# Sums of the out projection's moving operand, made two slices a step beside seventeen attention steps

## The chip, the cores and the metric

The kernel runs on one core of one Trainium2 chip. The metric is the device time of one execution in microseconds (us). Profiles come from the hardware profiler: they name TensorE (PE, with its weight loads as PEld), VectorE (DVE), ScalarE (ACT), GpSimd (POOL) and SyncE (SP), whose queue issues nearly all DMAs of this kernel.

## The reference, cut to what matters

One layer over 2048 tokens of width 1024, all in float32: a token mixer, a cross attention and a feed-forward block, each between two RMS norms. The mixer is what matters here:

```python
u = rms_norm(h, g_mix_pre[l])
z = u @ w_in[l]
qa, ka, va, qh, fh, ih, gh = jnp.split(z, IN_SPLITS, axis=-1)
ya = swa_with_sinks(qa, ka, va, sinks[l])          # sliding-window attention, 8 heads
yh = hgrn2(qh, fh, ih, gh, lb, hgrn_onorm[l])      # gated linear recurrence, 4 heads
y = jnp.concatenate([ya, yh], axis=-1) @ w_out[l]  # the out projection
h = h + rms_norm(y, g_mix_post[l])
```

(The reshapes are left out.) The kernel has to give the same result to within float32 accuracy, so it splits each operand of a large product into a high and a low part and sums three products.

## The kernel before, in words

**Large products.** They run mostly by a scheme that makes seven products of half-size blocks instead of eight (as in Strassen's). For it, sums and differences of the four quarters of the moving operand are needed. For the weights `w_out` of the out projection the program makes these sums once, ahead of time, and stores them in DRAM, in `out_s`; the products' stage later reads them back with `row<-out_s`.

**The sums.** `sums` (L1395) returns the DRAM tile and a generator over `combined` (L1025). For each of two halves of a quarter, `combined` makes four operands (keys 5, 7, 6, 4): it loads halves of the quarters of `w_out` (L75, called from `w_out`, L1388; the upper quarters as two DMAs of 64 partitions), yields three times, makes one `tensor_tensor` of 128 x 1024 on VectorE (L1032), issues the store to `out_s` (L78) and yields once more. That is two halves x four operands x four slices = 32 slices with eight sums, twelve loads of tiles of 512 KB and eight stores of 512 KB. A slice is what one `next` advances. The loads go into tiles `u` (two buffers) and `x` (three buffers) of the pool `io`. The same tiles `u` and `x` hold the decays of the recurrence (L718 to L721, `decays` at L724) for the four columns of the forget gate.

**The order of the work around the change.** Function `mix` interleaves generators by hand. `swa` (L964) gives one attention step of 128 tokens at each `next`, seventeen in all: the front of step n (loads of queries `qd`, keys `kr` and values `vr` from `z_d`, their split, scores, softmax) and the back of step n-1 (transposes, product with the values, store to `y_d`). `hgrn` (L946) gives one pair of chunks of the recurrence. `cols` (`in_proj`, L682) gives one column block of the in projection for the second half of the tokens: 48 matmuls of 128 x 512 (L156 to L158) and an eviction to a tile `z`, which is stored to `z_d`. A first loop of nine turns takes one attention step, one pair of the recurrence and one column each. A second loop takes the remaining eight attention steps and one column each. Then `fold_cross` (the folded weights of the cross attention) runs beside the remaining pairs of the recurrence, and the products begin.

**Who sets the final order.** The program is recorded in this order and then rearranged: the tile framework is asked to schedule the instructions of each engine (`schedule_with_timeline_sim=True`), so that an instruction can be issued earlier or later than the loops name it. What it keeps is the order of dependent instructions and the buffers: a tile of a pool with two buffers waits until the tile two before it is no longer used. Within an engine, and within SP's queue of DMAs, instructions then run strictly in the scheduled order: one that waits holds up all behind it. Queries have two buffers (`qd`, `qs`), keys one (`kr`, `kh`, `kl`).

The names that the text uses: `qs` (L768 on ACT, L769 on DVE) are the split queries; `kh` and `kl` (L987, L988, called at L779) the split keys; L803 and L804 the score matmuls; L808 the masked minimum, L812 the exponential, L823 the normalization; `pth`/`ptl` (L841, L842) the split transposed probabilities, L846 and L847 their product with the values; L732, L738 and L752 the decays.

Of the kernel before, what the change touches and what calls it, by code (L numbers as in the profile page):

```python
# [48 lines left out]
class Layer:  # L49
# [144 lines left out]
    def mix(self):  # L194
        tc, I = self.tc, self.I
        kw = dict(reuse_waits="tile")
        with contextlib.ExitStack() as left:
            def pool(name, at, **k):
                return at.enter_context(tc.tile_pool(name=name, bufs=1, **k, **kw))

            self.mc = pool("mc", left)
            self.r_x = self.cst.tile([P, NT], F32, name="r_x")
            with (
                tc.tile_pool(name="t1", bufs=3, **kw) as self.ts,
                tc.tile_pool(name="t2", bufs=3, **kw) as self.tb,
                tc.tile_pool(name="s1", bufs=2, side="right", **kw) as self.st_pool,
                contextlib.ExitStack() as at,
            ):
                self.banks(at, "ps1", **MOST)
                self.raws = 3  # L210
                u = self.in_first()
            self.banks(left, "ps2", **FOUR)
            self.hg = pool("hg", left)
            self.wp = pool("wp", left)
            self.io = pool("io", left)
            with tc.tile_pool(name="sw", bufs=1, side="right", **kw) as self.sw:
                self.zero_tiles()
                swa = self.swa(range(NT), lambda n: "st" if n < NPB else "sth")
                hgrn = self.hgrn(range(NPB), "h")
                cols = self.in_proj(1, u)  # L220
                next(cols)
                for _ in range(NPB + 1):
                    next(swa)
                    next(hgrn)
                    next(cols)
                for _ in hgrn:
                    pass
                self.out_sums, side = self.sums("out_s", self.w_out, 4, lambda: self.io_tile("u"), lambda: self.io_tile("x"))
                side = side()
                next(side)  # L230
                pairs = self.hgrn(range(NPB, NT), "gt")
                for i, _ in enumerate(swa, NPB + 2):
                    next(cols)
                    if i == NT + 1 - 0:
                        next(pairs)
                    for _ in range(4):
                        next(side, None)
                for _ in cols:
                    pass
            phases = self.phases(self.jobs(), None, lambda: self.io_tile("z"))  # L240
            with tc.tile_pool(name="xp", bufs=1, side="right", **kw) as self.xp:
                fold = self.fold_cross()
                for _ in range(2):
                    next(fold)
                for i, _ in enumerate(pairs, 1):
                    for _ in range(2):
                        next(fold)
                    if 2 <= i < 10:
                        next(phases)
                for _ in fold:  # L250
                    pass
            left.close()
            with (
                tc.tile_pool(name="t3", bufs=3, **kw) as self.ts,
                tc.tile_pool(name="t4", bufs=3, **kw) as self.tb,
                tc.tile_pool(name="s3", bufs=2, side="right", **kw) as self.st_pool,
                contextlib.ExitStack() as at,
            ):
                self.banks(at, "ps3", **MOST)
                self.raws = 4  # L260
                for _ in phases:
                    pass
# [1502 lines left out]
```

## Time and profile before

| what | before |
|---|---|
| median of three runs | 2584.7 us (2578.32 to 2585.96) |
| the profiled execution's own time | 2583.14 us |
| its span, first to last instruction | 2581.4 us |
| mean granted TensorE clock | 0.997 |
| attention with the columns beside it | about 267 to 632 us of the span |
| folded cross attention and remaining recurrence | about 632 to 820 us |

A profile lists instructions by the line of the kernel that made them, the engine, the operation and its tiles (`out<-in`). "Busy" is the union of an engine's instruction spans; matmuls are pipelined, so a busy TensorE may or may not be at its full rate. A wait row names who waited, for whom, the total in us, how often, and the longest. A row of a timeline gives start, duration, engine, line, operation, tiles and count, and in brackets the idle time before it with what ended it. A row of the DMA list gives the count, the size of one and the median time from issue to landing. A row of busy time by stretch gives the stretch, its length, each engine's busy us and count, the granted clock, the mean busy share of the 16 DMA engines and the GB/s they moved.

### The profile page before, as it was taken

What the parts mean: (1) busy time and instruction counts of PE and PEld (TensorE: products, weight loads), DVE (VectorE), ACT (ScalarE), POOL (GpSimd) and SP (SyncE); (2) the same over time, 40 slices, a digit from 0 to 9 for tenths busy, and PEclk for the clock granted to TensorE, in tenths of its full rate; (3) what the DMA queues carried; (4) which work ended last, traced back from release to release, by engine and by line L of the source; (5) the groups of instructions that cost most, each with busy time, mean ns of one, the idle gap of its engine ahead of it and who ended that gap; (6) DMA issues with size and microseconds to landing.
All of it is one profiled execution on the core that took longest, in us unless ns stands there. A gap on an engine that the chain in (4) does not pass through costs nothing.

```text
span 2581.4 us, 34890 instructions
## 1 busy us (share of the span) xinstructions
PE 2540.2 (98%) x12326; PEld 2127.1 (82%) x12326; DVE 1765.3 (68%) x2791; ACT 1262.4 (49%) x2643; POOL 422.6 (16%) x612
## 2 busy tenths in 40 slices
PE   9999999999999999999999999999999999999998
PEld 8888888888988778888778888888888888888886
DVE  7785588987556778778885655566666557574766
ACT  5563466565555565565563333354333335453543
POOL 5231334321302232212300000000000000000022
PEclk9999999999999999999999999999999999999999
DMA  6445755765887886666973622253565425464886
GB/s 188 147 163 178 198 164 158 239 186 175 251 279 283 295 274 217 211 228 200 325 246 127 208 87 74 89 189 130 172 203 196 156 93 190 158 199 106 224 178 152
DMA packets 357295, 486.36 MB, mean 188 GB/s; under 512 B 20352, under 2 KB 248704, under 8 KB 357120
## 3 DMA queue, kind: packets, MB, share of 16 engines
q1 hardware_dynamic: 351072, 462.11, 54.7%
q0 software_dynamic: 6048, 22.02, 4.9%
q8 instruction: 97, 1.59, 0.3%
q14 instruction: 78, 0.64, 0.1%
HBM read 317.34 MB, written 166.72 MB: 188 GB/s over the span
## 4 chain that ended last, share of the span: by engine, by line
PE 83%; DMA 6%; DVE 5%; ACT 3%; issue 2%; SPq 0%; POOL 0%; DVEq 0%; POOLq 0%; ACTq 0%
PE psm L1122 23%; PE psm L1124 23%; PE psm L1123 23%; PE psg L158 2%; PE psg L157 2%; PE psg L156 2%; PE pss L1381 1%; ACT T L985 1%; DMA h1t_d<-row 1%; DMA raw<-in_wo_x_dram 1%; DVE S L988 1%; DMA x<-in_w_out_dram 1%; DMA z<-in_w_out_dram 1%; DMA kk<-z_d 0%; ACT junk L1476 0%
## 5 line engine op out<-in xcount | busy, mean ns | idle before, releaser
L1122 PE MATMUL psm<-T,S 128*128 128x512 f32 x2680 | 1038.3, 392 | 11.4 <-ACT part L1137 9.9
L1123 PE MATMUL psm<-T,S 128*128 128x512 f32 x2680 | 1043.9, 390 | 0.9 <-DVE T L988 0.8
L1124 PE MATMUL psm<-T,S 128*128 128x512 f32 x2680 | 1031.0, 390 | 4.4 <-DVE S L988 4.4
L1122 PEld LDWEIGHTS psm<-T,S 128*128 128x128 f32 x2680 | 504.0, 188 | 120.5 <-ACT part L1137 10.2
L1124 PEld LDWEIGHTS psm<-T,S 128*128 128x128 f32 x2680 | 503.7, 188 | 111.0 <-DVE S L988 6.1
L1123 PEld LDWEIGHTS psm<-T,S 128*128 128x128 f32 x2680 | 504.3, 188 | 105.4 <-DVE T L988 2.3
L985 ACT ACTIVATE S<-sum 128x512 fp32r<-128x512 f32 (+1 forms) x330 | 198.4, 618 | 364.4 <-PE psm L1124 269.5
L988 DVE TENSOR_TENSOR S<-sraw,S 128x512 fp32r<-128x512 f32 (+1 forms) x315 | 214.1, 687 | 227.9 <-ACT S L985 214.2
L988 DVE TENSOR_TENSOR S<-sum,S 128x512 fp32r<-128x512 f32 (+1 forms) x388 | 260.5, 680 | 44.9 <-ACT S L985 29.4
L1137 ACT ACTIVATE part<-psm 128x512 f32<-128x512 f32 x285 | 168.7, 596 | 242.4 <-PE psm L1124 222.6
L985 ACT ACTIVATE S<-sraw 128x512 fp32r<-128x512 f32 (+1 forms) x268 | 165.3, 618 | 105.1 <-PE psm L1124 95.1
L1509 POOL DMA_DIRECT2D y_d<-row x16 | 14.0, 876 | 1076.5 <-DVE row L1695 1025.3
L988 DVE TENSOR_TENSOR T<-row,T 128x1024 fp32r<-128x1024 f32 (+1 forms) x112 | 132.5, 1195 | 40.7 <-ACT T L985 40.4
L157 PE MATMUL psg<-u,whi 128*128 128x512 f32 x320 | 127.8, 399 | 0.0
L158 PE MATMUL psg<-u,wlo 128*128 128x512 f32 x320 | 127.1, 397 | 0.0
L156 PE MATMUL psg<-u,whi 128*128 128x512 f32 x320 | 127.1, 397 | 0.0
L1476 ACT ACTIVATE junk<-row 128x512 f32<-128x512 f32 x160 | 99.7, 624 | 52.3 <-DVE row L1498 31.8
L985 ACT ACTIVATE T<-row 128x1024 fp32r<-128x1024 f32 (+1 forms) x112 | 114.0, 1032 | 17.4 <-DMA row<-d_s 6.6
L987 POOL TENSOR_SCALAR S<-sum 128x512 fp32r<-128x512 f32 x58 | 51.7, 891 | 299.1 <-PE psm L1124 247.1
L1646 DVE TENSOR_TENSOR row<-psm,part 128x512 f32<-128x512 f32 x66 | 43.7, 688 | 68.4 <-PE psm L1124 68.4
L1655 DVE TENSOR_TENSOR part<-psm,part 128x512 f32<-128x512 f32 x66 | 43.8, 688 | 62.7 <-PE psm L1124 62.5
L1695 DVE TENSOR_TENSOR row<-psm,part 128x512 f32<-128x512 f32 x72 | 49.1, 688 | 51.1 <-PE psm L1124 51.0
(364 smaller groups left out, 3710.4 us busy)
## 6 DMA issues: line engine op xcount, KB each, us to landing
sraw<-in_w_gate_dram SPq DMA_DIRECT2D x44, 512.0 KB, 3.6
sraw<-in_w_up_dram SPq DMA_DIRECT2D x44, 512.0 KB, 3.6
hid_d<-row SPq DMA_DIRECT2D x44, 512.0 KB, 2.7
sraw<-hid_d SPq DMA_DIRECT2D x32, 512.0 KB, 4.1
sraw<-in_w_in_dram SPq DMA_DIRECT2D x44, 256.0 KB, 3.4
z_d<-pair SPq DMA_DIRECT2D x20, 512.0 KB, 2.9
raw<-in_w_in_dram SPq DMA_DIRECT2D x20, 512.0 KB, 4.9
z_d<-z SPq DMA_DIRECT2D x20, 512.0 KB, 3.7
```

Source lines behind the costliest of these rows:

```text
L156: nc.tensor.matmul(ps, ah, bh, start=(i == 0), stop=False)
L157: nc.tensor.matmul(ps, ah, bl, start=False, stop=False)
L158: nc.tensor.matmul(ps, al, bh, start=False, stop=(i == n - 1))
L985: self.nc.scalar.activation(hi, raw, AF.Copy)
L987: self.nc.gpsimd.tensor_scalar(hi, raw, 1.0, 1.0, ALU.mult, ALU.mult)
L988: self.nc.vector.tensor_tensor(lo, raw, f32(hi), ALU.subtract)
L1122: nc.tensor.matmul(ps, s[:, 0, k, :], t[:, 0, k, :], start=st, stop=False, **kw)
L1123: nc.tensor.matmul(ps, s[:, 0, k, :], t[:, 1, k, :], start=False, stop=False, **kw)
L1124: nc.tensor.matmul(ps, s[:, 1, k, :], t[:, 0, k, :], start=False, stop=sp, **kw)
L1137: nc.scalar.activation(t, ps, AF.Copy)
L1476: self.nc.scalar.activation(junk, a, AF.Square, scale=float(D) ** -0.5, accum_out=to)
L1695: nc.vector.tensor_tensor(d, a, b, ALU.add)
```

## The change

The generator of the sums is made before the first loop, not between the two loops; it is advanced two slices at each of the nine turns of the first loop (18 slices) and two slices at each turn of the second (the rest), where before it was advanced four slices at each turn of the second loop alone.

```diff
                 cols = self.in_proj(1, u)
+                self.out_sums, side = self.sums("out_s", self.w_out, 4, lambda: self.io_tile("u"), lambda: self.io_tile("x"))
+                side = side()
+                next(side)
                 next(cols)
                 for _ in range(NPB + 1):
                     next(swa)
                     next(hgrn)
+                    for _ in range(2):
+                        next(side, None)
                     next(cols)
                 for _ in hgrn:
                     pass
-                self.out_sums, side = self.sums("out_s", self.w_out, 4, lambda: self.io_tile("u"), lambda: self.io_tile("x"))
-                side = side()
-                next(side)
                 pairs = self.hgrn(range(NPB, NT), "gt")
                 for i, _ in enumerate(swa, NPB + 2):
                     next(cols)
                     if i == NT + 1 - 0:
                         next(pairs)
-                    for _ in range(4):
+                    for _ in range(2):
                         next(side, None)
```

The sums, their loads and stores, and all other work are the same in number and shape. Because two lines are added, every line behind the edit has a number two higher in the changed kernel.

## The prediction

> **What bounds the kernel now.** I read the page first, then busy time by stretch, TensorE's waits in each stretch, and the sums' own rows with the DMA list and SP's timeline. The page's head and its first part:
>
> ```profile
> span 2581.4 us, 34890 instructions
> PE 2540.2 (98%) x12326; PEld 2127.1 (82%) x12326; DVE 1765.3 (68%) x2791; ACT 1262.4 (49%) x2643; POOL 422.6 (16%) x612
> ```
>
> TensorE (PE) is busy for 2540.2 of 2581.4 us. A matmul's span overlaps its neighbour's, so the rate is read from starts:
>
> ```profile
> 449.93 0.39 PE L157 MATMUL psg<-u,whi 128*128 128x512 f32 x1
> 450.16 0.39 PE L158 MATMUL psg<-u,wlo 128*128 128x512 f32 x1
> ```
>
> One 128x512 matmul takes 0.39 us but the next starts 0.23 us later: the column matmuls of the in projection run back to back. The edit keeps every matmul, so it acts only through time in which PE stands still. Busy time by stretch: the attention before the sums, the stretch in which the sums run, the rest of the attention, and the handover to the folded cross attention:
>
> ```profile
> core 0: us, PE busy (x) PEld busy (x) DVE busy (x) ACT busy (x) POOL busy (x), PEclk, DMA share, GB/s
> 267.00:440.00 173.00, 171.72 (x995) 148.81 (x994) 128.81 (x332) 103.12 (x316) 63.62 (x102) 1.00 0.58 169
> 440.00:540.00 100.00, 97.59 (x524) 81.38 (x523) 89.20 (x193) 60.63 (x166) 35.55 (x51) 1.00 0.83 244
> 540.00:632.00 92.00, 90.61 (x489) 76.84 (x487) 71.50 (x183) 54.23 (x143) 13.87 (x29) 1.00 0.44 137
> 632.00:820.00 188.00, 181.04 (x1245) 165.82 (x1246) 103.05 (x138) 100.96 (x224) 39.43 (x50) 1.00 0.81 264
> ```
>
> PE idles 173.00 - 171.72 = 1.28 us, then 100.00 - 97.59 = 2.41, then 1.39, then 6.96. VectorE (DVE) is busy 74% of the first stretch and 89% of the second, where the DMA engines move 244 GB/s instead of 169. So the sums stand in the fuller half, but they disturb PE little there. Who PE waited for from 440 to 540 us, and then from 267 to 440:
>
> ```profile
> PE psh L847 <- DVE ptl L842: 1.0, 2, 0.7
> PE pst L837 <- DVE ptl L842: 0.7, 1, 0.7
> PE pss L837 <- DVE w_mn L808: 0.5, 1, 0.5
> PE pst L837 <- DVE w_mn L808: 0.2, 1, 0.2
> ```
>
> ```profile
> PE pst L804 <- DVE kl L988: 0.7, 1, 0.7
> PE pss L803 <- DVE vst L789: 0.5, 1, 0.5
> ```
>
> All of it is DVE being late: 2.4 us beside the sums, 1.2 us before them.
>
> **The change part by part.** Nothing is added or removed: eight sums (L1032), their loads of w_out and eight stores of out_s move. The sums' own rows, and the row of the stage that reads what they store:
>
> ```profile
> L1032 DVE TENSOR_TENSOR u<-u,x x6: 1207/1221/1225, 451.2 to 525.4; 128x1024 f32<-128x1024 f32 x6
> L1032 DVE TENSOR_TENSOR x<-x,u x2: 1206/1216/1225, 499.2 to 527.1; 128x1024 f32<-128x1024 f32 x2
> ...
> L75 SPq DMA_DIRECT2D row<-out_s x8: 319/352/597, 782.6 to 804.6; - x8
> ```
>
> Eight sums at 1.22 us are 9.8 us of DVE, all of it now between 451 and 527 us. The result is read from 782.6 us on, so no reader is late or early: storing it sooner is worth nothing by itself.
>
> *The late steps.* The order in which the changed program's instructions stand puts three sums beside the first three steps, one at the sixth, one at the eighth or ninth and three around the twelfth. At least four leave the crowded stretch: 4 x 1.22 = 4.9 us, which takes DVE there from 89.2 to about 84.3 of 100. PE's 2.4 us of waiting is the bound of the gain; the other bound is 0, if those waits come from the softmax chain alone. Only half the sums go: I take half, **-1.2 us**.
>
> *The entry.* This is where something gets worse. The changed order places four w_out issues on SP's queue ahead of the first queries, and a fifth, with the first store, ahead of the second step's. SP's timeline at the entry, and the rows that show what issues of w_out take:
>
> ```profile
> 270.84 0.51 SPq L75 DMA_DIRECT2D sg<-z_d  x1
> 271.39 2.66 SPq L75 DMA_DIRECT2D qd<-z_d  x4
> 274.09 1.26 SPq L75 DMA_DIRECT2D kr<-z_d  x2
> 275.40 0.59 SPq L75 DMA_DIRECT2D vr<-z_d  x1
> 278.89 2.58 SPq L75 DMA_DIRECT2D qd<-z_d  x4
> 281.58 0.57 SPq L75 DMA_DIRECT2D kr<-z_d  x1
> ...
> 441.25 1.26 SPq L75 DMA_DIRECT2D x<-in_w_out_dram  x2
> 442.56 1.25 SPq L75 DMA_DIRECT2D u<-in_w_out_dram  x2
> ```
>
> Four issues are 1.26 + 1.25 = 2.5 us, by which the first queries, keys and values come later. What they feed, on DVE (first two rows) and on PE (last two):
>
> ```profile
> 278.18 0.69 DVE L769 SCALAR_TENSOR_TENSOR qs<-qd,qs 64x512 fp32r<-64x512 f32 x1 [7.59 <-ACT qs L768]
> 291.46 0.69 DVE L988 TENSOR_TENSOR kl<-kr,kh 128x512 fp32r<-128x512 f32 x1 [3.78 <-POOL kh L987]
> ```
>
> ```profile
> 281.44 0.33 PE L804 MATMUL pst<-kl,qs 128*128 128x128 f32 x1 [0.73 <-DVE kl L988]
> 294.60 0.28 PE L804 MATMUL pst<-kl,qs 128*128 128x256 f32 x1
> ```
>
> The first score matmuls wait 0.73 us today. In the changed order 68 column matmuls stand ahead of them, not 50: 18 x 0.23 = 4.1 us more cover against 2.5 us more delay, so that wait goes: -0.7. The first sum stands ahead of the first qs on DVE, and queries, keys and scores queue behind it; by a landing time of 5.6 us (row below) its w_out is in at about 271.4 + 2.5 + 5.6 = 279.5, in DVE's idle 7.59 us, and it ends as the shifted qs becomes ready at 278.18 + 2.5 = 280.7: 0, at most 1.2. The cover taken there is missing at the second step: its scores stand behind 96 column matmuls in both orders, and its kl was done at 291.46 + 0.69 = 292.15, 2.4 us ahead of the matmul at 294.60. Delay 2.5 + 0.6 (the fifth issue), less 2.4 of slack, plus the 0.7 by which PE arrives sooner: 1.4. In all **+0.7 us**, between -0.7 (only the first wait goes) and 3.1 + 1.2 = +4.3 (nothing covers).
>
> A rule of the skill speaks against the change here. The Trainium skill, Perfetto Trace Analysis, section "What "DMA-bound" means", counts as DMA-bound a stretch in which the issuing engine's track is solid with DMA slices; SP's rows at the entry have gaps under 0.1 us from 270.84 to 275.99, so it agrees with the form, while PE's single 0.73 us wait there says the bound is still PE.
>
> *The rest of the first nine steps.* A store of out_s waits on SP for its sum, and the next steps' loads wait behind it. SP's and DVE's waits from 440 to 540 us, then the landing times there, then the queries' landing time from 267 to 440:
>
> ```profile
> SPq L78 <- DVE u L1032: 9.9, 4, 4.1
> ```
>
> ```profile
> DVE u L1032 <- DMA out_s<-u: 1.7, 1, 1.7
> ...
> DVE u L1032 <- DMA x<-in_w_out_dram: 0.8, 1, 0.8
> ```
>
> ```profile
> x<-in_w_out_dram SPq DMA_DIRECT2D x12, 256.0 KB, 5.6
> ...
> qd<-z_d SPq DMA_DIRECT2D x18, 128.0 KB, 3.9
> ```
>
> ```profile
> qd<-z_d SPq DMA_DIRECT2D x39, 128.0 KB, 3.2
> ```
>
> In the late steps such stores held SP for 9.9 us in four waits and DVE stood 2.5 us before its sums, and still PE lost only 2.4 us; queries landed in 3.9 us instead of 3.2. The early steps have DVE at 74%, so more slack. I take **0**, between 0 and +9.9 (every held us reaches PE). The tiles u and x are shared with the decays; in the changed order the decay scans keep their places within a step, and their columns are read only from about the twelfth step on, so a late tile costs 0 unless it holds a column's matmuls.
>
> *The handover.* Load order there changes too (k and kk of the next recurrence pairs). It holds PE's largest idle time, 6.96 us; I find no reason for a sign: **0**, between -7.0 and +7.0.
>
> Sum: -1.2 + 0.7 + 0 + 0 = -0.5 us. The profiled execution took 2583.14 us, 2581.4 of it span: 2582.6. The median of the three runs is 1.6 us higher; I state **2583**, between 2582.6 and 2584.7 - 0.5 = 2584.2.
>
> **The rivals.** *SP's issuing bounds the entry.* If the solid SP track is what ends last, all five added issues come through: 5 x 0.63 = 3.2 us, 2586.3 us. For it: the four early issues stand ahead of everything the first step needs. Against it: 18 more column matmuls. (By the rule of the Trainium skill above this would be the result; the trace bears it out in form only.)
>
> *Slower: stores of out_s hold the early steps' loads.* Each of four stores blocks SP's queue until its sum is made, and queries, keys and values of the next step are issued behind it. It decides once a step's loads come later than PE's cover, 2.4 us at the second step. If the 9.9 us measured late reach PE early, the time is 2583.1 + 9.9 = 2593.0, and 4 x 4.1 = 16.4 us at worst, 2599.5. For it: keys have a single buffer, so no step can fetch far ahead. Against it: the late steps, with DVE fuller, let through only a quarter.
>
> *Faster: the disturbance goes with the crowding.* If the late stretch loses all its 2.41 us and the new load order also takes the handover's 6.96, the time is 2583.1 - 9.4 = 2573.7. For it: both stand beside full DMA queues (0.83 and 0.81 busy). Against it: the handover's loads are its own, not the sums'.
>
> *The sums don't move at all*, because the recorded order is rearranged afterwards: excluded, since the first store of out_s stands ahead of the second step's queries in the changed order.
>
> **How the numbers follow.** Forecast 0.51, own range 2578 to 2588 (its terms' bounds, without the held stores and the handover); SP's issuing 0.13; held stores 0.22; faster 0.14. About 0.3% (7.8 us) is what a measurement of this kernel can tell from no change. The forecast and the SP rival lie within it, 0.64; held stores beyond it, 0.22; the faster rival 0.14. The range runs from 2574 (the faster rival's time) to 2598 (held stores, short of their worst) and leaves out about 0.08 below and 0.11 above. Nearly all cases lie close, because PE idles for only 12 us in 553.
>
> **What would show it.** Late steps: DVE from 440 to 540 us at about 84%, PE's wait there near 1.2 us, x<-in_w_out_dram landing faster than 5.6 us. Entry: the first score's wait gone, a new one of 1 to 2 us at the second step's scores. Held stores: waits of SP on L1032 between 270 and 400 us, and PE waits on kl, qs or vst behind them; the forecast fails if these pass 3 us. The handover fails me if PE's idle time from 632 to 820 us differs from 7 us by more than 3. A gain or loss after 820 us would be none of my terms.

## The result, and the profile after

| what | before | after |
|---|---|---|
| median of 10 runs each | 2582.64 us (2577.73 to 2585.96) | 2590.34 us (2585.79 to 2596.99) |
| ratio, 95% interval | | 1.0030 [1.0018, 1.0042] |
| profiled execution, its own time | 2583.14 us | 2591.59 us |
| mean granted TensorE clock in it | 0.997 | 0.995 |

The change costs 7.7 us, 0.3% (by the interval 4.6 to 10.8 us). The ratios in the tables are not quotients of the medians, so that the two can differ by a microsecond or two.

The head of the page after, then its busy time by stretch (columns as in the table of before: PE, PEld, DVE, ACT, POOL busy, granted clock, DMA share, GB/s). Lines behind the edit have numbers two higher: the sum is L1034 now.

```profile
span 2589.9 us, 34898 instructions
...
PE 2546.1 (98%) x12326; PEld 2131.9 (82%) x12326; DVE 1767.1 (68%) x2791; ACT 1260.8 (49%) x2643; POOL 429.7 (17%) x612
```

```profile
267.00:440.00 173.00, 166.09 (x929) 141.58 (x928) 129.85 (x313) 94.58 (x287) 62.38 (x95) 0.99 0.70 199
440.00:540.00 100.00, 98.96 (x556) 84.32 (x555) 88.10 (x200) 63.83 (x181) 38.80 (x56) 1.00 0.59 183
540.00:632.00 92.00, 92.00 (x488) 78.05 (x487) 71.02 (x189) 54.63 (x150) 14.93 (x30) 1.00 0.41 129
632.00:820.00 188.00, 181.37 (x1254) 167.35 (x1253) 100.72 (x137) 101.13 (x222) 40.68 (x51) 0.98 0.80 261
```

PE now idles 173.00 - 166.09 = 6.91 us in the first stretch (before 1.28), then 1.04 (2.41), 0 (1.39) and 6.63 (6.96). So the late stretches give back 2.8 us, the handover does not move, and the first stretch takes 5.6. PE's busy sum of the whole span rises by 5.9 us as well (2546.1 against 2540.2), for the same 12326 matmuls: that is time at a lower clock (0.995 in place of 0.997 is 5.2 us of the span), to which the text comes back.

To see where it is lost, each matmul of after was matched with the same one of before (by its line and its count) and the starts in the two timelines subtracted:

| matched matmul (its start in before) | lag of after |
|---|---|
| column ahead of the attention (272 us) | -0.3 us |
| third step's first score (314 us) | +4.1 |
| fourth step's (334 us) | +3.9 |
| eighth step's (430 us) | +10.6 |
| last columns (590 us) | +6.3 |
| in the handover (720 us) | +9.5 |
| first products (826 us) | +6.3 |
| last products (2435 us) | +7.4 |

Where matmuls of different kinds changed places the lag jumps a little for that alone, so points at which both kernels begin the same work (826 us) are firmer than those between. Most is lost by 430 us and part of it is won back; the handover loses and regains some 3 us, and little happens behind 826 us. Each lag compares one profiled execution with one other, and late in the span executions also differ by some us without the change (e1, below, goes from -1.1 us at 826 to -4.9 us at 2435 us), so lags are used for the entry above all.

**The entry.** SP's timeline of after, from the first added load on:

```profile
271.12 0.75 SPq L75 DMA_DIRECT2D x<-in_w_out_dram  x1
271.91 1.27 SPq L75 DMA_DIRECT2D u<-in_w_out_dram  x2
273.23 0.60 SPq L75 DMA_DIRECT2D x<-in_w_out_dram  x1
273.88 2.58 SPq L75 DMA_DIRECT2D qd<-z_d  x4
277.18 1.64 SPq L75 DMA_DIRECT2D kr<-z_d  x2
```

The order is the forecast one: four loads of 256 KB ahead of the first queries, which are issued 2.5 us later. The DMA list gives the median time from issue to landing of a step's four query loads. First the first step's, before (267 to 276 us) and after (267 to 279 us); then the second step's, before (276 to 283 us) and after (281.9 to 288 us):

```profile
qd<-z_d SPq DMA_DIRECT2D x4, 128.0 KB, 5.3
```

```profile
qd<-z_d SPq DMA_DIRECT2D x4, 128.0 KB, 6.8
```

```profile
qd<-z_d SPq DMA_DIRECT2D x4, 128.0 KB, 2.8
```

```profile
qd<-z_d SPq DMA_DIRECT2D x4, 128.0 KB, 5.6
```

Issued later, they also travel longer, 1.5 us in the first step and 2.8 us in the second. In the first step 2.5 + 1.5 = 4.0 us are close to the time of the bytes ahead of them: 1.05 MB at the 247 GB/s of the stretch from 267 to 300 us are 4.2 us, an estimate. ACT, which makes the high part of the queries, shows both: its waits for them from 267 to 312 us, before and after (total, times, longest).

```profile
ACT qs L768 <- DMA qd<-z_d: 4.1, 2, 3.8
```

```profile
ACT qs L770 <- DMA qd<-z_d: 15.6, 3, 8.2
```

The first step hides all but 0.4 us of it behind the columns (PE waits that long for `vr`). The second does not: DVE's and PE's timelines of after, then PE's busy time there in pieces of 3 us.

```profile
296.74 1.23 DVE L1034 TENSOR_TENSOR u<-u,x 128x1024 f32<-128x1024 f32 x1 [1.56 <-DMA x<-in_w_out_dram]
...
301.82 0.21 DVE L791 TENSOR_TENSOR vst<-pss,vst 128x64 fp32r<-128x64 f32 x1
```

```profile
299.70 0.39 PE L157 MATMUL psg<-u,whi 128*128 128x512 f32 x1
302.18 0.55 PE L805 MATMUL pss<-kh,qs 128*128 128x256 f32 x1 [2.10 <-DVE vst L791]
302.53 0.41 PE L806 MATMUL pss<-kl,qs 128*128 128x256 f32 x1
...
303.17 0.63 PE L158 MATMUL psg<-u,wlo 128*128 128x512 f32 x1
303.60 0.63 PE L156 MATMUL psg<-u,whi 128*128 128x512 f32 x1
```

```profile
300.00:303.00 3.00, 0.90 (x5) 0.85 (x5) 2.91 (x15) 1.85 (x6) 0.07 (x1) 0.86 1.14 304
303.00:306.00 3.00, 3.00 (x12) 2.53 (x12) 2.54 (x4) 1.52 (x6) 2.02 (x3) 0.58 1.15 279
```

PE stands 2.10 us, and then its next 3.4 us run at half clock: column matmuls start 0.43 us apart in place of 0.23, and the clock column reads 0.86 and 0.58 (0.14 x 3 + 0.42 x 3 = 1.7 us lost). 2.1 + 1.7 = 3.8 us; the new 0.4 us of the first step and the 0.7 us that went there make it 3.5. The lag grows from -0.3 to +4.1 us, so that some 0.9 us are not in these rows. On this view alone the culprit seems to be the sum at 296.74, which stands in DVE's queue, after a wait of its own for `x`, ahead of what makes the values. The experiments show that it is not needed for a loss, though such sums have a part in it.

**The fourth to eighth step.** PE's waits of after from 380 to 405 and from 405 to 432 us (before, it was busy for all of the first and for 26.45 of the 27 us of the second):

```profile
PE psh L913 <- DVE sg L944: 1.1, 1, 1.1
PE psg L156 <- DVE z L713: 0.7, 1, 0.7
```

```profile
PE psh L913 <- DVE sg L944: 1.0, 1, 1.0
PE psh L902 <- ACT atz L888: 0.9, 1, 0.9
```

Small waits, mostly for DVE, in steps that have decays and sums side by side.

### The profile page after: what moved, and what is told of

It reads as the page before. It is cut to its first block, busy times and chain, and to the rows that moved or that the text cites. A ratio compares the mean times of both kernels' runs of the same rounds, so it can differ in the third digit from the quotient of the medians.

```text
span 2589.9 us, 34898 instructions
## 1 busy us (share of the span) xinstructions
PE 2546.1 (98%) x12326; PEld 2131.9 (82%) x12326; DVE 1767.1 (68%) x2791; ACT 1260.8 (49%) x2643; POOL 429.7 (17%) x612
## 4 chain that ended last, share of the span: by engine, by line
PE 84%; DMA 6%; DVE 4%; ACT 3%; issue 2%; SPq 1%; POOL 1%; DVEq 0%; POOLq 0%; ACTq 0%
PE psm L1124 23%; PE psm L1125 23%; PE psm L1126 23%; PE psg L156 2%; PE psg L158 2%; PE psg L157 2%; PE pss L1383 1%; DMA u_d<-row 1%; ACT T L987 1%; DMA h1t_d<-row 1%; DMA raw<-in_wo_x_dram 1%; SPq L75 1%; ACT junk L1478 0%; PE pss L839 0%; DMA row<-y_d 0%
```

## The experiments

The first four ask which turns are to blame and whether SP's queue carries the loss. From e5 on, theory A says that DVE, standing in order at its first two sums, brings the entry's softmax chain late; rival B says that the loads do it, and e9 and e10 split B into their bytes (C) and their place in SP's queue (D).

| kernel | median, us | before, timed beside it | ratio [95%] |
|---|---|---|---|
| e1 sums from the fifth turn | 2581.17 | 2581.85 | 0.9997 [0.9987, 1.0008] |
| e2 sums at the first four turns, then late | 2587.50 | 2581.85 | 1.0021 [1.0010, 1.0031] |
| e3 loads of the sums on ACT's queue | 2597.10 | 2581.85 | 1.0059 [1.0044, 1.0074] |
| e4 late only, five slices a turn | 2582.32 | 2581.85 | 1.0001 [0.9991, 1.0011] |
| e5 no additions | 2590.83 | 2584.56 | 1.0019 [1.0009, 1.0029] |
| e6 additions on GpSimd | 2603.57 | 2584.56 | 1.0073 [1.0061, 1.0085] |
| e7 sums from the third turn | 2582.50 | 2584.56 | 0.9995 [0.9986, 1.0003] |
| e8 twice the slices at the first four turns | 2599.78 | 2584.56 | 1.0059 [1.0044, 1.0073] |
| e9 an eighth of the bytes, no additions | 2582.19 | 2581.02 | 1.0003 [0.9993, 1.0013] |
| e10 before, with copies at the entry | 2592.76 | 2581.02 | 1.0038 [1.0026, 1.0050] |
| e11 sums from the second turn | 2588.06 | 2581.02 | 1.0026 [1.0013, 1.0039] |

**Which steps: e1, e2 and the control e4.** Only the slices of each turn change; on the left the first loop with its turn k, on the right the second, and the slice ahead of the loops is dropped:

```diff
-   for _ in range(2):                                       for _ in range(2):
+e1 for _ in range(2 if k > 3 else 0):                       for _ in range(3):
+e2 for _ in range((3 if k == 0 else 2) if k < 4 else 0):    for _ in range(4):
+e4 for _ in range(0):                                       for _ in range(5):
```

> The sums begin at the fifth of the nine turns of the first loop (two slices a turn there, then three a turn in the second loop), so nothing of w_out is loaded at the entry. If the entry is to blame (the loads of w_out on SP's queue ahead of the first steps' loads), the third step's first score matmul is no longer 4.1 us late against the kernel before, and the time falls by about 4 us from the changed kernel's 2590.3 to about 2586. If the sums beside the decays at the fifth to ninth turns are to blame, the entry's share is small and the 6.5 us lost between 360 and 430 us stay: about 2589. If any new order costs several us by chance, it can land anywhere from 2580 to 2592.

> Slices at the first four turns only (two each, three at the first), none beside the decays of the first loop, the rest four a turn in the second loop as before. If the entry is to blame, the third step is again 4 us late and the time is about 2587 or above. If the stretch beside the decays is to blame, the time is near the kernel before, about 2583, whatever the entry shows.

> The control for a mere new order: as the kernel before, the sums only beside the second loop, but five slices a turn instead of four (and made with no first slice ahead of it). Every theory that blames the first loop's sums expects 2582 to 2584, the time of the kernel before. If any new order moves this kernel by several us, this one is off by 3 us or more in either direction.

e1 and e4 are level with before (e1 goes beyond the 2586 us that were expected of the entry alone), e2 has most of the loss. In e2 the third step is 4.2 us late as in the changed kernel, and the lag then stays near 4 to the eighth step, where the changed kernel's rises to 10.6. So the first four turns are to blame, and a shuffled order as such (e4) costs nothing. PE's wait in e2, and the sum that stands on DVE ahead of what PE waits for:

```profile
301.39 0.36 PE L804 MATMUL pss<-kh,qs 128*128 128x256 f32 x1 [1.48 <-DVE vst L790]
```

```profile
298.95 1.23 DVE L1033 TENSOR_TENSOR u<-u,x 128x1024 f32<-128x1024 f32 x1 [4.69 <-DMA x<-in_w_out_dram]
```

DVE stands 4.69 us until w_out has landed, and the second step's minimum and values come behind it. ACT's wait for queries is longer too (9.9 us from 267 to 320 us), so both a held DVE and late queries are at work in e2.

**SP's queue: e3.** The changed kernel with the sums' loads issued by ScalarE:

```diff
+            load = self.load
+            if name == "out_s":
+                self.load = self.nc.scalar.dma_start
             src(t, i, j, k0, n)
+            self.load = load
```

> The changed kernel with the sums' loads of w_out issued on ACT's DMA queue in place of SP's; stores and everything else stay. If SP's queue is what carries the loss (a DMA on it waits for the landing of the one eight places earlier, and all behind it wait), the third step is on time and the time comes back to about 2583 to 2585. If VectorE is what carries it (it stands 12.1 us ahead of three sums until w_out has landed, and has 1.2 us more work a sum), the loss stays: about 2590.

It is slower than either expectation, and slower than with the loads on SP: off SP's queue they still hurt, third step 9.4 us late, fourth 11.9. PE's waits from 267 to 330 us:

```profile
PE pst L849 <- DVE ptl L844: 4.9, 1, 4.9
PE pss L786 <- DMA vr<-z_d: 2.5, 2, 1.6
```

The Trainium skill, DMA: Bandwidth & Descriptors, section "Issuing engines are not separate DMA queues", says that DMAs begun by different engines run on the same DMA engines and interleave; the trace agrees, since values land later though SP issues fewer transfers (6.1 us from issue to landing from 267 to 300 us, 3.6 before). ACT's own lateness is mixed into e3's time (its first eviction of a column, at 273.13 us before, comes at 277.00 us, behind four of these issues; the profile names the landing of `sg` for that wait), so e3 clears SP's queue as sole carrier and does no more.

**The additions: e5 and e6.** e5 leaves out the eight additions (so `out_s` holds unsummed quarters) and keeps loads and stores; e6 makes them on GpSimd.

```diff
 e5:
-                with self.behind():
-                    nc.vector.tensor_tensor(t, t, o, op)
+                if dst is not self.out_sums:
+                    with self.behind():
+                        nc.vector.tensor_tensor(t, t, o, op)
 e6:
+                if dst is self.out_sums:
+                    nc.gpsimd.tensor_tensor(t, t, o, op)
+                else: ...
```

> The changed kernel with the eight additions on VectorE left out (its loads of w_out and its eight stores stay, so out_s holds quarters that are not summed; 8 x 1.22 = 9.8 us less VectorE work). Theory A, VectorE standing in order at the first two sums and so coming late to the second step's normalization, minimum and values: the 4.1 us by which the third step's scores come late are gone, lag there within 0.7 us of the kernel before, time 2581 to 2584 us. Rival B, the loads themselves (their place in SP's queue or the DMA engines that they keep full) make queries and values late: the third step stays about 4 us late, time 2586 to 2590 us. A part of both: lag 1 to 3 us, time 2584 to 2586.

> The changed kernel with the eight additions made on GpSimd in place of VectorE. GpSimd makes kh for every step, so a sum that waits there for its load holds the keys. Theory A (an engine that stands in order at a sum that has not landed hands its wait on to the softmax chain): the loss does not go but moves, scores wait for kh or kl from the second step on; an addition of 128x1024 there will take longer than 1.22 us, I put it at 2 to 3 us; time 2586 to 2596. Rival B (loads): third step about 4 us late as in the changed kernel, with waits on vr and vst, time 2588 to 2591. If VectorE alone was the carrier and GpSimd has the room: 2581 to 2584.

With no addition left, the third step is 2.5 and the fourth 6.7 us late, and ACT waits for queries as long as in the changed kernel. e5's ACT from 267 to 312 us and PE from 267 to 340 us:

```profile
ACT qs L770 <- DMA qd<-z_d: 15.2, 3, 8.6
```

```profile
PE pss L839 <- DVE w_mn L810: 2.5, 1, 2.5
PE pss L805 <- DVE vst L791: 0.9, 1, 0.9
PE pss L786 <- DMA vr<-z_d: 0.9, 1, 0.9
```

The 2.5 us follow from another late load, at the fourth step. POOL's timeline of e5, then DVE's:

```profile
319.26 0.61 POOL L894 TENSOR_TENSOR kk<-kk,G 128x256 f32<-128x256 f32 x1 [7.69 <-DMA kk<-z_d]
...
323.36 1.05 POOL L989 TENSOR_SCALAR whi<-raw 128x1024 fp32r<-128x1024 f32 x1
```

```profile
324.44 1.22 DVE L990 TENSOR_TENSOR wlo<-raw,whi 128x1024 fp32r<-128x1024 f32 x1 [6.13 <-POOL whi L989]
```

POOL stands for the recurrence's `kk`, DVE for the column weights that POOL splits behind it, the softmax behind DVE, and PE for the softmax. Theory A as the whole cause falls: PE still waits for DVE, but DVE has no sum to stand at and is itself fed late. The third step's 2.5 us in place of 4.1 is what was expected of a part of both, so the sums are not cleared. What does go without the additions is the second loss: e5's lag stays at 6.7 from the fourth to the eighth step. e6 keeps the entry's loss (6.3 at the fourth step) and adds others: an addition on GpSimd takes 2.4 to 3.4 us, PE stands 4.9 us from 500 to 540 us, and the clock reads 0.92 from 632 to 700 us. It came out 8 us beyond its expected range, and I did not follow that further.

**How far from the entry, and how much: e7, e11, e8.** e7 is e1 with `k > 1`, e11 with `k > 0`; e8 is e2 with 5, 4, 4, 4 slices.

> Sums begun at the third turn, two slices a turn, then three a turn in the second loop: nothing of them beside the first two attention steps. If only the entry is at fault (the first two steps, which have no steps ahead of them to give slack): scores on time, 2580 to 2583 us, as with the start at the fifth turn (2581.2). If sums beside any early step cost, each about the same: of the changed kernel's 7.7 us some 3 to 5 stay, 2585 to 2587 us.

> Sums begun at the second turn (two slices a turn, then three a turn in the second loop): no load of w_out ahead of the first step's queries, 0.5 MB ahead of the second's, about 1.5 MB ahead of the third's. Beginning at the third turn cost nothing, beginning at the first 4 us. Theory C (bytes up to the third step decide): 1 to 3 us late at the third or fourth step, 2583 to 2587 us. Rival: only the four loads ahead of the first step's queries cost: on time, 2581 to 2583 us.

> Twice the slices at the first four turns (5, 4, 4, 4 in place of 3, 2, 2, 2), none at turns five to nine, four a turn from then on. The same with single slices there was 5.5 us slower than before, third step 4.2 us late. If the loss goes with the number of sums and loads at the entry: third or fourth step 7 to 9 us late, 2590 to 2595 us. If only the first landing costs (what is queued behind the first two sums): still 4 to 5 us late, 2586 to 2589 us.

Begun at the third turn the sums cost nothing (fourth step 0.1 us early), at the second 2.8 us at the fourth step, at the first 3.9. Twice the slices there bring 7.6. e11's time lies just above its range, with a wide interval; e8's lies above its range, because it loses nearly 8 us more between the fourth step and the products.

The schedule did not follow the turns closely. In e2, e7 and e11 SP issues all loads of the first step ahead of the first load of w_out; ahead of the second step's queries stand 1 MB in e2 and 0.5 MB in both e7 and e11, and e7 makes its first sum at 295.95 us, so it is not free of sums beside the first two steps. What differs is the dose: from 267 to 300 us e7 issues 1.0 MB of w_out, e11 2.0, the changed kernel 2.25, e2 2.5. "Only the four loads ahead of the first queries" (e11's rival) does not hold, since e2 and e11 lose and have none there.

But e11 does not speak for late queries either. ACT waits for them no longer than before, and PE waits for what stands on DVE behind two sums. ACT's wait (267 to 312 us), then PE's second wait and the sum ahead of `W` on DVE:

```profile
ACT qs L769 <- DMA qd<-z_d: 3.9, 2, 3.6
```

```profile
307.46 0.92 PE L885 MATMUL psh<-qq,k 128*128 128x192 f32 x4 [1.44 <-DVE W L914]
```

```profile
304.74 1.22 DVE L1033 TENSOR_TENSOR u<-u,x 128x1024 f32<-128x1024 f32 x1 [3.17 <-DMA x<-in_w_out_dram]
```

So the entry's loads cost on two paths: they make the steps' own loads late (e5, without any sum), and the sums that wait for them hold DVE (e11, with queries in time). The changed kernel and e2 have both, and no run parts their shares.

**Bytes or place: e9 and e10.** e9 keeps every load and store of the sums, with an eighth of the rows, and leaves out the additions; the other rows of `out_s` are filled beside the last eight steps from `z_d`, so it does not hold the sums. e10 is the kernel before with six copies of 512 KB from DRAM to DRAM that nothing reads.

```diff
 e9:
+            m = p // 8 if small else p
-            self.load(d, self.I["w_out"][...].rearrange("(k p) d -> p k d", p=p))
+            self.load(d[:m], self.I["w_out"][...].rearrange("(k p) d -> p k d", p=p)[:m])
 e10:
                 for k in range(NPB + 1):
+                    for s, (c, t) in enumerate(at[k] if k < 3 else ()):
+                        self.store(spare[2 * k + s], self.z_d[c:c + P, t:t + TB])
```

> The changed kernel with its sums' loads and stores at the same places and as many, but of an eighth of the rows, and without the additions (the other rows of out_s are filled beside the last eight steps from z_d, so out_s does not hold the sums). Theory C, the bytes: the DMA engines, 0.77 busy from 267 to 300 us before and 0.98 in the changed kernel, are what makes queries and values land late (qd 6.0 us against 4.1): with an eighth of them the share there is below 0.85, qd lands in 4 to 4.5 us, the third and fourth step's scores are within 1 us of the kernel before, time 2580 to 2584 us. Rival D, the place in SP's queue (five issues more ahead of the first two steps' queries, stores that wait on SP): third and fourth step 3 to 7 us late as without the additions (2.5 and 6.7), time 2586 to 2590 us.

> The kernel before, its sums where they were, with six added copies of 512 KB from DRAM to DRAM (z_d to a scratch tensor that nothing reads), two ahead of the queries of the first step, two beside those of the second, two beside those of the third: 3 MB of traffic, and no tile, addition or later transfer that depends on it. Theory C (bytes): share near 1 from 267 to 300 us, qd lands in about 6 us, third or fourth step 4 to 7 us late, time 2586 to 2592 us. Rival D (order, held stores, tiles shared with the decays): six short issues, below 1 us late, 2581 to 2584 us.

They part bytes from mere place well, if not wholly. ACT's waits for queries from 267 to 312 us, e9 and then e10:

```profile
ACT qs L773 <- DMA qd<-z_d: 4.9, 2, 4.2
```

```profile
ACT qs L773 <- DMA qd<-z_d: 15.8, 4, 7.0
```

e9 has nearly before's wait (4.1) with as many issues as the changed kernel; e10 has the changed kernel's (15.6) with only added traffic and no sum or tile. Busy time by stretch at the entry, of before, then e9, then e10:

```profile
267.00:300.00 33.00, 32.27 (x169) 27.56 (x168) 15.98 (x52) 13.52 (x45) 11.16 (x18) 1.00 0.77 207
```

```profile
267.00:300.00 33.00, 32.89 (x171) 28.02 (x170) 11.49 (x37) 11.14 (x36) 9.41 (x16) 1.00 0.70 201
300.00:330.00 30.00, 30.00 (x172) 26.10 (x172) 24.22 (x74) 17.68 (x59) 9.20 (x16) 1.00 0.66 196
```

```profile
267.00:300.00 33.00, 30.67 (x151) 25.56 (x149) 7.43 (x28) 9.41 (x31) 6.47 (x11) 1.00 0.84 238
300.00:330.00 30.00, 27.58 (x145) 24.01 (x146) 19.69 (x58) 14.54 (x50) 11.02 (x18) 0.89 0.80 201
```

In e9 PE idles 0.1 us in 63, and from the columns ahead of the attention to the fourth step it gains 0.6 us on before (its profile was 3.8 us late already ahead of the entry, where nothing was changed; that is subtracted). In e10 PE idles 2.3 + 2.4 us, and its clock falls to 0.89 over 30 us, which is 6.6 us at half clock; some 5.6 us of these fall on matmuls and lose half of that, 2.8. Less before's 0.73 this makes 6.8, and the lag by the fourth step grows by 11.2 - 3.8 = 7.4. Its time lies just above the range of C. So bytes ahead of and beside the queries are enough for the entry's loss, and without additions an eighth of them costs nothing where all of them do (e5); D, the place in the queue alone, falls. Three limits remain. e9's four issues ahead of the first queries are also shorter (0.45 + 0.81 + 0.30 = 1.56 us, in the changed kernel 2.62), and its fifth load and first store were scheduled behind the second step's queries, so it does not keep every place; but e10 loses 7.4 us behind four copies that take SP only 1.22 + 1.75 = 3.0 us to issue. In e10 SP itself stood 0.9 + 1.3 + 1.8 us from 275 to 300 us until copies had landed, and 1.3 + 1.2 us for w_out in the changed kernel (270 to 283 us), so the bytes delay by the travel of the data and by holding the queue, and the runs do not part these two. And no run has the additions with an eighth of the bytes, which would price the sums alone. The share of busy DMA engines is a poor measure of the loss: e7 shows 0.93 from 267 to 300 us without loss, e10 0.84 with it.

## Why the prediction was wrong, point by point

- **The entry, +0.7 us, is the step that failed.** The order, the 2.5 us of issuing, the vanished first wait and "1 to 2 us new wait at the second step's scores" (2.10) came as said, and the first sum was a microsecond later than forecast (280.51 to 281.74, its end due at 280.7). But the wait came by another path than the one worked out: `kl` was done at 293.31 + 0.69 = 294.00 us, 1.9 us later than before and within its 2.4 us of slack, and PE waited for the values `vst`, so that the size of the forecast wait was luck. Three things were missing from the sum. The delay of the queries was taken as issue time alone, with the landing left as it was; it grew from 5.3 to 6.8 us in the first step and from 2.8 to 5.6 us in the second, and e9 and e10 show that the bytes, and not the issuing alone, are what costs. Only the first sum was priced, while the second stood on DVE ahead of the values. And the wait was priced at its own length, while 3.4 us at half clock followed it, 1.7 us more. In all 4.1 us at the third step, where the bound was +4.3. (The own range, 2578 to 2588, does not follow from its terms: -2.4 - 0.7 and +4.3 us give 2580.0 to 2587.4.)
- **The rest of the first nine steps, 0, was wrong too, by another mechanism than the one feared.** SP waited for sums only 1.1 + 0.8 us between 270 and 400 us:

```profile
SPq L78 <- DVE x L1034: 1.1, 1, 1.1
...
SPq L78 <- DVE u L1034: 0.8, 1, 0.8
```

  So the rival of the held stores falls. But PE's lag grows by 6.7 us from the fourth to the eighth step. PE stands 4.2 us from 360 to 432 us there against 0.6 before, so some 3.7 us of this are lost time, and the rest is matmuls that changed places. In these profiles it comes only with additions (none in e5) at these turns (none in e2) and a late entry (e1 has sums there, an entry in time and no loss); why is not shown. How much of it is left at the end is open: the ratios of e2 and of the changed kernel overlap.
- **The late steps, -1.2 us, fit.** PE's idle time there fell by 1.4 us, and by as much again from 540 to 632 us. DVE did not fall to 84% (88.10): the stretch held more of the other work (556 matmuls in place of 524). e1 and e7, which have this gain without the entry's loss, are level with before: it is too small to be told.
- **The handover, 0, was right** in idle time (6.63 against 6.96). In the profile of after one wait of 3.2 us stands there and the clock reads 0.88 from 632 to 660 us, some 3.4 us lost; before has more of its waits later (3.1 us from 740 to 780 us, after 0.9), so that the lag rises to 9.5 us and falls back. e4, which is no slower than before, shows the same 0.88 at that place, so I do not count it to the change. But then 3.4 of the 6.3 us by which this one profile is late at 826 us are not the change's, and the 7.7 us rest on the medians, not on this pair of profiles.
- **The rival "SP's issuing bounds the entry"** (2586.3 us) came nearest in time and was wrong in its mechanism: e10 loses 7.4 us behind four issues of 3.0 us, and e9 has as many issues, if shorter ones, and loses nothing. The rule of the Trainium skill behind it (Perfetto Trace Analysis, "What "DMA-bound" means") knows a second case, the DMA engines themselves; the trace of before had them 0.77 busy from 267 to 300 us, and the prediction read only the other.

## What to carry to other kernels

Before putting transfers into a stretch, look at who else's data is in flight there: a load that nobody waits for delayed those behind it by about the time of its bytes (4.0 us for 1 MB here), and the first two steps of this stage had too little slack to hide it. The same holds for an instruction that waits for such a load in order: what stands behind it waits too. Moving the loads to another engine's queue did not make them free (e3); beginning two turns later did (e7). And give a wait of TensorE a second price, for the case that the clock falls behind it.

## What the runs showed of the hardware

A short wait of TensorE can be followed by half clock, but its length alone does not decide. The 2.10 us of the changed kernel were followed by 3.4 us at half clock, and so were 2.5 us in e5 (0.94 from 300 to 330 us); the 1.48 us of e2 and the 1.96 us of e6 at the same matmul were not (1.00 there). Yet in the products one and the same matmul waits 2.42 us in both kernels, with full clock behind it before and half clock after. First before, then after, the matmul and the stretch around it:

```profile
893.31 0.51 PE L1124 MATMUL psm<-T,S 128*128 128x512 f32 x1 [2.42 <-DVE S L988]
890.00:900.00 10.00, 7.58 (x35) 6.01 (x34) 9.77 (x11) 3.98 (x9) 3.86 (x5) 1.00 0.93 325
```

```profile
899.58 0.79 PE L1126 MATMUL psm<-T,S 128*128 128x512 f32 x1 [2.42 <-DVE S L990]
896.00:906.00 10.00, 7.58 (x30) 5.91 (x29) 8.68 (x10) 3.65 (x8) 2.82 (x4) 0.83 0.95 331
```

The 0.17 x 10 = 1.7 us lost there are again 3.4 us at half clock. So the 1.7 us behind the entry's wait may be chance in part, and other executions of the changed kernel may not have them. The Trainium skill, TensorE: Matmul & The Clock Gate, section "Part 1: The HAM clock gate (the "warmup" mystery)", puts the fall to half clock behind an idle window of about 3.4 us, and the return behind a busy window of that length. The length of the slow piece agrees; the idle time that brought it on was shorter here.
